# Hybrid streaming encoder, two layers on one core: PSUM tiles from a ring, mixer weights split once and reread as pairs, and a new order of work

## The chip, the core and the metric

The kernel runs on one core of a Trainium2 chip. A core has five engines with queues of their own: TensorE (PE, matmuls; its weight loads are listed as PEld), VectorE (DVE), ScalarE (ACT), GpSimdE (POOL) and SyncE (SP), which here issues every DMA. Matmul results land in PSUM, eight banks of 128 x 512 float32; everything else lives in SBUF or in DRAM. The metric is the time of one execution in device microseconds. The time before is 2417.01 us, the median of three runs (2414.57 to 2417.25).

## What is computed

Two layers run over nine tiles of 128 rows: tiles 0 to 7 are a prompt of 1024 rows, tile 8 holds 8 running streams of 16 rows ("sample"). Model width 1024, feed-forward width 2816 (22 tiles of 128). Cut to what matters here:

```python
def trunk_layer(x, ...):
    xn = rms_norm(x, norm_mix)
    q, k, v, u = split(xn @ w_in)            # 512 | 128 | 128 | 512 columns
    q, k = rope(rms_norm(q)), rope(rms_norm(k))
    attn = sink_attention(q, keys, vals)     # prompt: 64-row chunks, window of 3 chunks
    pool = pool_mixer(u) @ w_pool * scale    # sliding means of 2, 4, 8, 16 rows
    x = x + concat(attn, pool) @ w_out
    h = rms_norm(x, norm_ffn) @ w_up         # 1024 -> 5632
    c = conv3(h)                             # three taps along the rows
    x = x + (silu(gate(c)) * val(c)) @ w_down
```

The sample's tile attends to a cache of 128 rows per stream as well as to its own 16. Rolling caches and states are outputs too.

## The kernel before, in words

All large products are made from float32 operands cut into two parts, hi (rounded to the format that PE reads fast) and lo (the rest): three matmuls, hi*hi, hi*lo and lo*hi (`mm3`, lines 172 to 175). A weight piece of 128 x 512 is loaded into one of five `raw` buffers, cast by ACT (L198) and subtracted by DVE (L199) into a tile of two halves, hi and lo. That is `w_split`.

Each layer has three stages.

- **Mixer.** The nine tiles go in three batches b of three. For each batch there are streams of units: `n` (norm and transposes, L266 to L293), `k` (q, k and v columns: 12 units, three accumulators), `u` (pooling columns: 8 units, two accumulators), `p` (pool matmuls, 4 units, L461), `o` (output projection: 16 units, three accumulators; its first four units and the same in the second half need only the pool part, the others the attention of the batch's three tiles), then `m` (norm for the feed-forward). Attention runs tile by tile as one chain of steps, `L`: preparation a1 to b3, scores, softmax, transposes and values. The sample's tile 8 comes last in that chain. Its step `qk` issues 24 small DMAs (rows of k and v to the outputs and to a tile at partition 0, L699 to L703). Every batch loads and splits the same weight pieces anew: 12 of `w_in` for k, 8 for u and 16 of `w_out`, 36 per batch and 108 per layer.
- **Up.** The up-projection is written as seven products per tile of columns (`PRODUCTS`) on sums and differences of quarters of the input and of the weight, for two halves s of the rows. The sums of the input (`sums(s)`, L325 to L334) are 7 splits and 4 additions of 128 x 1152 per half. `up_post` adds the products up out of PSUM (L943), convolution and gate follow (L990 to L1002), and the result goes to DRAM (`gd`).
- **Down.** In three chunks of the inner dimension, the w_down pieces are split once (`down_prep`, L1044 to L1046) and stay in SBUF. For each of the nine tiles `down_load` fetches the activations from `gd` (L1053), casts and subtracts them (L1055, L1056) and fetches the running x (L1058). The last chunk of layer 0 runs into the mixer of layer 1 (tokens `d`).

What sets the order. A planner (`arrange`) sorts the mixer's steps ("tokens") by keys in a table `PLAN` and takes them in that order as far as their predecessors are done and limits on buffers are kept: among them `mm`, at most four accumulators open at a time. In this list a step's place is its priority; the framework then orders each engine's queue by a schedule of its own in which a step goes as soon as its inputs and buffers are there, the earlier step of the list first. SP's queue, too, is in order: a DMA that waits holds all behind it. `w_advance` asks for weight splits ahead of their unit: two units ahead, four (`LA = 4`) in the middle of the list, where three pieces of seven go into one of the 33 big `B` buffers (`wide`) and the others into five `W` buffers; raw loads go five pieces ahead. Before, the eight PSUM banks are one tile, and the program picks the bank itself: 0 to 3 taken and given back by accumulators (`mm_take`, `mm_give`), 4 and 5 in turn for scores, values and down (`s`), 6 and 7 in turn for transposes and the pool matmuls (`tr`). Up uses banks 0 to 5 as three pairs, one half of the rows in each bank of a pair, and one instruction reads both halves (128 x 576).

Of the kernel before, what the change touches and what calls it, by code (L numbers as in the profile page):

```python
# [17 lines left out]
LA = 4  # L18
# [11 lines left out]
class Weight:  # L30
    def __init__(self, load, n=512, split=True):
        self.load, self.n, self.split, self.wide, self.ahead, self.dve = load, n, split, False, 2, False
# [12 lines left out]
def arrange(tokens, limits):  # L45
# [4 lines left out]
    while left:  # L50
# [7 lines left out]
        for r, n in t.res.items():  # L58
# [7 lines left out]
    dict(k0=(-37.12, 1.06), u0=(-19.58, 1.84), k1=(29.16, 2.63), u1=(73.67, 4.61), o0=(87.72, 2.71),  # L66
         k2=(154.86, 0.47), u2=(167.69, 3.03), o1=(176.8, 5.19), o2=(244.18, 3.8), p0=(39.27, 6.38),
         p1=(90.02, 4.48), p2=(191.64, 17.42), n1=(-29.42, 1.49), n2=(23.54, 3.88), n3=(91.98, 1.07),
         m0=(213.68, 1.15), m1=(240.36, 0.87), m2=(284.99, 1.11), d=(-23.94, 1),
         L=(26.9, 49.72, 64.52, 77.21, 108.8, 144.26, 156.17, 180.28, 202.35, 239.71), cw=(247.35, 4.51),  # L70
         sc=(270.55, 7.25), e_q=1, e_k=0, e_v=0, e_u=0, e_k2=0, e_qt=0, e_pt0=0, e_pt1=0, e_ps0=1, e_ps1=1,
         e_ks=1, e_w=0, e_x0=1, e_x1=0, e_x2=0),
# [11 lines left out]
def encoder_kernel(ctx: ExitStack, tc: tile.TileContext, consts, x_prompt, x_sample, cache_k, cache_v,  # L84
# [15 lines left out]
    BUFS = dict(B=33, W=5, raw=5, PT=4, Q=4, u=2, sA=1, sB=1, D=2, V=5, st=15, ks=1)  # L100
# [17 lines left out]
    psum = ps.tile([128, 8, 512], F32, name="psum")  # L118
    turn = {"s": [4, 5], "tr": [6, 7]}
    mmfree = [0, 1, 2, 3]  # L120

    def P(tag):

        b = turn[tag].pop(0)
        turn[tag].append(b)
        return psum[:, b]

    def mm_take():
        return mmfree.pop(0)
# [21 lines left out]

    state = {}
# [33 lines left out]
    def w_dma(w):  # L186
        w.raw = raw_tile(w.n)
        w.load(w.raw)

    def w_split(w):  # L190
        if not w.split:
            return
        g = T("B" if w.wide else "W", [128, 2, 512], F32R)
        w.hi, w.lo = g[:, 0, 0:w.n], g[:, 1, 0:w.n]
        if w.dve:
            dve.tensor_copy(out=w.hi, in_=w.raw)
        else:
            act.copy(out=w.hi, in_=w.raw)  # L198
        dve.tensor_tensor(out=w.lo, in0=w.raw, in1=f32(w.hi), op=ALU.subtract)  # L199
        w.raw = None  # L200

    def w_advance(pos):
        upto, more = pos + 1, 0
        while upto < len(order) and more < min(order[pos].ahead, order[upto].ahead):
# [139 lines left out]
    def kvq_units(l, b):  # L344
        us = []
        for c, (cols, kn, n) in enumerate(((0, 1, 512), (512, 2, 256))):
            hold = {}
            for j in range(8 // kn):
                def f(w, c=c, kn=kn, n=n, j=j, hold=hold):
                    xT = state["xT", b]  # L350
                    wh, wl = [v.rearrange("p (k n) -> p k n", k=kn) for v in (w.hi, w.lo)]
                    for tl in range(3):
                        t = b * 3 + tl
                        if j == 0:
                            hold[tl] = mm_take()
                        o = psum[:, hold[tl], 0:n]
# [4 lines left out]
                        if (j + 1) * kn == 8:  # L361
# [7 lines left out]
                            mm_give(hold[tl])  # L369
# [3 lines left out]
    def u_units(l, b):  # L373
        us = []
        for c in range(2):
            hold = {}
            for j in range(4):
                def f(w, c=c, j=j, hold=hold):
                    xT = state["xT", b]
                    wh, wl = [v.rearrange("p (k n) -> p k n", k=2) for v in (w.hi, w.lo)]  # L380
                    for s in range(2):
                        if j == 0:
                            hold[s] = mm_take()
                        for kk in range(2):
# [3 lines left out]
                            mm3(psum[:, hold[s], 0:384], a, x, j == 0 and kk == 0, j == 3 and kk == 1)  # L388
                        if j == 3:
                            u_evac(l, b, 2 * c + s, psum[:, hold[s]])  # L390
                            mm_give(hold[s])
# [956 lines left out]
```

## Time and profile before

| | |
|---|---|
| Median of three runs | 2417.01 us |
| Profiled execution | 2412.6 us, its span 2410.8 us |
| PE busy | 2280.5 us, 95% |
| PEld busy | 2025.8 us, 84% |
| DVE busy | 1596.4 us, 66% |
| ACT busy | 959.7 us, 40% |
| Mean granted clock of PE | 0.969 |
| DMA | 271.77 MB, 113 GB/s on average, all on SP's queue but 0.4% of the 16 engines' time |

Busy shares are averages over stages with different limits, so the table of stretches (busy time of each engine between two times, with the granted clock and the DMA engines' share) says more than this one. A matmul's listed duration includes its way through the pipeline; how fast matmuls follow each other is read from their count in a full stretch. The layers lie so: mixer 0 to about 455 us, up to 930, down to about 1215; the same again for layer 1, whose mixer begins under the end of layer 0's down and lasts to about 1645, up to 2121, down to the end.

### The profile page before, as it was taken

To read this page: it belongs to the slowest core of one execution; us is meant where nothing else is said; L and a number is where in the kernel's file an instruction comes from. 1 tells how busy PE (TensorE), PEld (TensorE's weight loads), DVE (VectorE), ACT (ScalarE), POOL (GpSimd) and SP (SyncE) were. 2 spreads that over 40 slices of the span, in tenths; PEclk is the share of its full clock that TensorE was granted. 3 is DMA by queue.
4 is the path that set the end of the run, shared out by engine and by line. 5 is a ranking of instruction groups with operands and counts; after the bars stand their busy time and mean duration, and the time that the engine had idled before them with its cause. 6 is when DMAs were issued, how large, how long until landed. Compare 5 with 4: busy or idle time off the path is not lost.

```text
span 2410.8 us, 35976 instructions
## 1 busy us (share of the span) xinstructions
PE 2280.5 (95%) x13610; PEld 2025.8 (84%) x13610; DVE 1596.4 (66%) x2942; ACT 959.7 (40%) x1774; POOL 201.6 (8%) x411
## 2 busy tenths in 40 slices
PE   7989979899999998999998899788999999989999
PEld 7757757899999997888887687578999999978887
DVE  5766665988888887233356776478888888853332
ACT  4555554534334334121236565454333433421110
POOL 0000000111111110000000000001111111100000
PEclk9989988899999999999999999889999999999999
DMA  6233332222222226364442333422222222273643
GB/s 218 62 112 122 99 117 89 84 79 70 79 75 71 77 75 225 131 218 164 143 135 61 99 127 102 133 89 65 65 80 78 69 79 75 79 246 125 222 157 109
DMA packets 244495, 271.77 MB, mean 113 GB/s; under 512 B 17410, under 2 KB 188370, under 8 KB 244290
## 3 DMA queue, kind: packets, MB, share of 16 engines
q1 hardware_dynamic: 244322, 269.48, 34.9%
q8 instruction: 107, 1.75, 0.3%
q14 instruction: 66, 0.54, 0.1%
HBM read 203.69 MB, written 67.42 MB: 112 GB/s over the span
## 4 chain that ended last, share of the span: by engine, by line
PE 82%; DVE 7%; DMA 5%; ACT 3%; issue 2%; SPq 1%; POOL 0%; ACTq 0%; DVEq 0%
PE psum L173 25%; PE psum L174 25%; PE psum L175 25%; PE psum L658 2%; DMA raw<-in_w_out_dram 2%; DVE W L199 1%; PE psum L305 1%; DVE B L326 1%; DMA raw<-in_w_in_dram 1%; PE psum L645 1%; DMA B<-gd 1%; DMA raw<-in_w_down_dram 1%; DVE B L334 1%; PE psum L461 1%; ACT W L198 1%
## 5 line engine op out<-in xcount | busy, mean ns | idle before, releaser
L173 PE MATMUL psum<-B,W 128*128 128x288 f32 (+1 forms) x1896 | 572.2, 302 | 18.3 <-ACT B L325 12.3
L174 PE MATMUL psum<-B,W 128*128 128x288 f32 (+1 forms) x1896 | 569.9, 301 | 8.1 <-DVE B L326 8.1
L175 PE MATMUL psum<-B,W 128*128 128x288 f32 (+1 forms) x1896 | 568.2, 300 | 0.0
L173 PEld LDWEIGHTS psum<-B,W 128*128 128x128 f32 x1896 | 359.4, 190 | 22.6 <-ACT B L325 13.9
L173 PE MATMUL psum<-B,B 128*128 128x512 f32 (+2 forms) x914 | 357.0, 394 | 20.1 <-ACT B L1055 10.3
L174 PEld LDWEIGHTS psum<-B,W 128*128 128x128 f32 x1896 | 358.8, 189 | 11.2 <-DVE B L326 10.2
L175 PEld LDWEIGHTS psum<-B,W 128*128 128x128 f32 x1896 | 358.9, 189 | 0.9 <-DVE W L199 0.5
L174 PE MATMUL psum<-B,B 128*128 128x512 f32 (+2 forms) x914 | 357.2, 391 | 0.0
L175 PE MATMUL psum<-B,B 128*128 128x512 f32 (+2 forms) x914 | 355.9, 391 | 0.0
L992 DVE SCALAR_TENSOR_TENSOR B<-B,cvp,B 128x1168 f32<-128x1168 f32 x176 | 250.5, 1428 | 7.9 <-ACT B L990 7.7
L173 PEld LDWEIGHTS psum<-B,B 128*128 128x128 f32 x914 | 172.9, 190 | 59.8 <-ACT B L198 11.5
L1083 DVE TENSOR_TENSOR B<-psum,B 128x512 f32<-128x512 f32 x108 | 74.5, 690 | 199.0 <-PE psum L175 198.9
L174 PEld LDWEIGHTS psum<-B,B 128*128 128x128 f32 x914 | 173.5, 190 | 37.6 <-DVE B L199 0.5
L175 PEld LDWEIGHTS psum<-B,B 128*128 128x128 f32 x914 | 172.8, 189 | 37.7 <-issue 0.2
L173 PE MATMUL psum<-W,B 128*128 128x512 f32 (+1 forms) x510 | 190.4, 386 | 9.5 <-ACT B L463 5.0
L199 DVE TENSOR_TENSOR W<-raw,W 128x512 fp32r<-128x512 f32 x184 | 125.8, 689 | 103.4 <-ACT W L198 102.7
L174 PE MATMUL psum<-W,B 128*128 128x512 f32 (+1 forms) x510 | 192.9, 379 | 0.9 <-DVE W L199 0.9
L868 ACT CAST W<-Q 128x512 fp32r<-128x512 f32 x132 | 81.8, 621 | 280.3 <-PE psum L175 280.1
L175 PE MATMUL psum<-W,B 128*128 128x512 f32 (+1 forms) x510 | 191.9, 381 | 0.0
L198 ACT CAST W<-raw 128x512 fp32r<-128x512 f32 x184 | 113.2, 620 | 166.9 <-PE psum L175 58.5
L943 DVE TENSOR_TENSOR B<-psum,PT 128x160 f32<-128x160 f32 (+2 forms) x356 | 147.8, 447 | 27.2 <-PE psum L175 27.1
L943 DVE TENSOR_TENSOR PT<-psum,PT 128x576 f32<-128x576 f32 (+1 forms) x138 | 100.4, 730 | 84.6 <-PE psum L175 84.3
(188 smaller groups left out, 3953.2 us busy)
## 6 DMA issues: line engine op xcount, KB each, us to landing
raw<-in_w_up_dram SPq DMA_DIRECT2D x176, 256.0 KB
xd<-B SPq DMA_DIRECT2D x63, 512.0 KB
B<-xd SPq DMA_DIRECT2D x63, 512.0 KB
raw<-in_w_in_dram SPq DMA_DIRECT2D x120, 256.0 KB
gd<-B SPq DMA_DIRECT2D x44, 576.0 KB
raw<-in_w_down_dram SPq DMA_DIRECT2D x88, 256.0 KB
B<-gd SPq DMA_DIRECT2D x36, 512.0 KB
raw<-in_w_out_dram SPq DMA_DIRECT2D x48, 256.0 KB
```

Source lines behind the costliest of these rows:

```text
L173: pe.matmul(out=out, lhsT=a[0], rhs=b[0], start=first, stop=False)
L174: pe.matmul(out=out, lhsT=a[0], rhs=b[1], start=False, stop=False)
L175: pe.matmul(out=out, lhsT=a[1], rhs=b[0], start=False, stop=last)
L198: act.copy(out=w.hi, in_=w.raw)
L199: dve.tensor_tensor(out=w.lo, in0=w.raw, in1=f32(w.hi), op=ALU.subtract)
L305: pe.transpose(out=tr[:, k * 128:(k + 1) * 128], in_=xn[:, c:c + 128], identity=ident)
L326: dve.tensor_tensor(out=lo, in0=src, in1=f32(hi), op=ALU.subtract)
L658: pe.matmul(out=o, lhsT=V, rhs=H.pop(("p", g, kk)), start=kk == kks[0], stop=kk == 1)
L868: act.copy(out=hi, in_=src)
L943: dve.tensor_tensor(out=o, in0=x, in1=y, op=ALU.add)
L992: dve.scalar_tensor_tensor(out=c, in0=h[:, j:j + 1168], scalar=cvp[:, j, ct:ct + 1], in1=c, op0=ALU.mult, op1=ALU.add)
L1083: dve.tensor_tensor(out=X[:, hs], in0=o, in1=X[:, hs], op=ALU.add)
```

## The change

- **Kept pairs.** Every split piece of k, u and o gets a key (layer, stream, index) and a DRAM tile `wsd[key]`. The first batch that needs it loads, casts and subtracts it as before and then stores the pair hi and lo (512 KB). The other two batches load the pair in one DMA straight into a `W` buffer: no raw load (256 KB), no cast, no subtract.
- **Buffers.** `W` has six buffers for five, `B` 32 for 33; `wide` is gone; the splits, and so the pair loads, are asked for three units ahead (`LA = 3`) throughout.
- **PSUM.** Each use of PSUM takes a tile of one bank from a pool with a tag: `mm` (4 banks), `s` (2), `tr` (2). The pool matmuls move from `tr` to `mm`. The planner has no `mm` limit any more. Up takes one tile for each half of the rows (the third product of three from `s`, the others from `mm`) and reads each half with an instruction of its own, so that each 128 x 576 read becomes two of 128 x 288.
- **Order.** In the attention chain tile 8 comes after tile 5, ahead of tiles 6 and 7; tile 6's preparation is spread over its last steps. All keys of `PLAN` are new, and the sums `s0`, `s1` and up's first weights (`upw`) have keys there. By these keys u2 and the start of o1 stand beside the sample's steps and tiles 6 and 7 beside o1; o2 begins before o1 ends; batch 0's o0 runs interleaved with u1; and up's first weights come last in the layer's list.
- **Up to down.** In up's last tile of columns `down_load` of the first tile is called at product 2, and not in the first down unit; `down_prep` of pieces 0 to 7 is spread over products 1 to 4 and not 0 to 3.

```diff
-LA = 4
+LA = 3
...
-    BUFS = dict(B=33, W=5, raw=5, PT=4, Q=4, u=2, sA=1, sB=1, D=2, V=5, st=15, ks=1)
+    BUFS = dict(B=32, W=6, raw=5, PT=4, Q=4, u=2, sA=1, sB=1, D=2, V=5, st=15, ks=1)
...
     def P(tag):
-        b = turn[tag].pop(0)
-        turn[tag].append(b)
-        return psum[:, b]
+        cnt[0] += 1
+        return ps.tile([128, 512], F32, tag=tag, name=f"{tag}{cnt[0]}", bufs={"mm": 4, "s": 2, "tr": 2}[tag])
...
+    wsd = {(l, x, i): dp.tile([128, 2, 512], F32, name=f"wd{l}{x}{i}")
+          for l in range(DEPTH) for x, n in (("k", 12), ("u", 8), ("o", 16)) for i in range(n)}
+    kept = set()
...
     def w_dma(w):
+        if w.key in kept:
+            return
         w.raw = raw_tile(w.n)
         w.load(w.raw)
...
-        g = T("B" if w.wide else "W", [128, 2, 512], F32R)
+        g = T("W", [128, 2, 512], F32R)
         w.hi, w.lo = g[:, 0, 0:w.n], g[:, 1, 0:w.n]
+        if w.key in kept:
+            sync.dma_start(out=f32(g), in_=wsd[w.key])
+            return
...
         dve.tensor_tensor(out=w.lo, in0=w.raw, in1=f32(w.hi), op=ALU.subtract)
         w.raw = None
+        if w.key is not None:
+            sync.dma_start(out=wsd[w.key], in_=f32(g))
+            kept.add(w.key)
...
-            o = P("tr")[:, 0:384]
+            o = P("mm")[:, 0:384]
             pe.matmul(out=o, lhsT=w.raw, rhs=d, start=True, stop=True)
...
+        seq = (0, 1, 2, 3, 4, 5, 8, 6, 7)
...
-            o = psum[:, 2 * pair + s, 0:QT]
+            o = state["upp", s] = P("s" if (7 * i + n) % 3 == 2 else "mm")[:, 0:QT]
...
+        for s in ss:
+            u = state.pop(("upp", s))
+            x = sum_("sum", s)
+            if n == 0:
+                act.copy(out=x, in_=u)
+            elif n == 1:
+                add(hb_first(row(0), s), [u], [x])
...
                     if i == FT - 1:
-                        for x in (2 * n, 2 * n + 1):
-                            if x < CHUNKS[0][1]:
+                        if n == 2:
+                            down_load(l, 0, 0)
+                        for x in (2 * n - 2, 2 * n - 1):
+                            if 0 <= x < CHUNKS[0][1]:
                                 down_prep(l, x)
...
-        ev = arrange(toks, {"T6": 18, "qkv": 4, "V": BUFS["V"], "mm": 4})
+        ev = arrange(toks, {"T6": 18, "qkv": 4, "V": BUFS["V"]})
```

More of the change, by code (lines that the diff above doesn't have):

```diff
@@ L31, in __init__ @@
     def __init__(self, load, n=512, split=True):
-        self.load, self.n, self.split, self.wide, self.ahead, self.dve = load, n, split, False, 2, False
+        self.load, self.n, self.split, self.dve, self.key = load, n, split, False, None
 class Unit:
@@ L65 @@
 PLAN = [
[L66 to L72, printed above, removed]
@@ L200, in w_split @@
         w.raw = None
+        if w.key is not None:
+            sync.dma_start(out=wsd[w.key], in_=f32(g))
+            kept.add(w.key)
     def w_advance(pos):
         upto, more = pos + 1, 0
-        while upto < len(order) and more < min(order[pos].ahead, order[upto].ahead):
+        while upto < len(order) and more < LA:
             if order[upto].layer != order[pos].layer:
@@ L354, in f @@
                         if j == 0:
-                            hold[tl] = mm_take()
-                        o = psum[:, hold[tl], 0:n]
+                            hold[tl] = P("mm")
+                        o = hold[tl][:, 0:n]
                         for kk in range(kn):
@@ L382, in f @@
                         if j == 0:
-                            hold[s] = mm_take()
+                            hold[s] = P("mm")
                         for kk in range(2):
@@ L387, in f @@
                             x = [xT[i][k // 3][:, k % 3, :] for i in range(2)]
-                            mm3(psum[:, hold[s], 0:384], a, x, j == 0 and kk == 0, j == 3 and kk == 1)
+                            mm3(hold[s][:, 0:384], a, x, j == 0 and kk == 0, j == 3 and kk == 1)
                         if j == 3:
-                            u_evac(l, b, 2 * c + s, psum[:, hold[s]])
-                            mm_give(hold[s])
+                            u_evac(l, b, 2 * c + s, hold[s])
                     if j == 3:
@@ L482, in f @@
                         if j == 0:
-                            hold[tl] = mm_take()
-                        o = psum[:, hold[tl]]
+                            hold[tl] = P("mm")
+                        o = hold[tl]
                         if k >= 4:
@@ L771, in pv @@
             state.pop(("qkv", 8))
-            state.pop(("V", 7))
             state.pop(("V", 8))
@@ L819, in L_steps @@
                 for i, f in enumerate(flat(rest[k])):
-                    put(t, f, (), **(mo if k == 3 and i == 0 else {}))
+                    put(p, f, (), **(mo if k == 3 and i == 0 else {}))
                 more(2 + k)
-            put(t, rest[4], (), **({"V": -1} if t else {}))
-        put(8, sloadv)
-        for f in srest[:-1]:
-            put(8, f)
-        put(8, srest[-1], (), qkv=-1, V=-2, T6=1)
-        kc1 = len(out) - len(srest) + 1
+            put(p, rest[4], (), **({"V": -2 if t == 7 else -1} if t else {}))
         return out, kc1
@@ L926, in up_post @@
     def up_post(l, i, n, ss):
-        pair = (7 * i + n) % 3
-        u = psum[:, 2 * pair:2 * pair + 2]
         last = 1 in ss
@@ L1197, in stream, with keyed @@
                 add(f"{st}.{i}", k + i * step, u, q, (res or {}).get(i))
+        def keyed(x, units, l=l):
+            for i, u in enumerate(units):
+                u.ws[0].key = l, x, i
+            return units
         if l == 0:
@@ L1254, in encoder_kernel @@
                 pre = ([f"s{s}.{i - 1}"] if i else []) + ([ready[i]] if i in ready else [])
-                add(f"s{s}.{i}", (246 if s == 0 else 290) + 3 * i, f, pre)
+                add(f"s{s}.{i}", pl[f"s{s}"][0] + pl[f"s{s}"][1] * i, f, pre)
         for i in range(3):
-            add(f"upw{i}", 286 + 6 * i, lambda l=l, i=i: up_advance(l, i), ["o2.10"])
-        ev = arrange(toks, {"T6": 18, "qkv": 4, "V": BUFS["V"], "mm": 4})
-        lim = [t.name for t in ev].index("spl")
-        wide = [w for t in ev[:lim] for w in t.unit.ws if w.split][12:]
-        for i, w in enumerate(wide[:-6]):
-            w.wide = i % 7 in (2, 4, 6)
-            w.ahead = LA
+            add(f"upw{i}", pl["upw"][0] + pl["upw"][1] * i, lambda l=l, i=i: up_advance(l, i), ["o2.10"])
+        ev = arrange(toks, {"T6": 18, "qkv": 4, "V": BUFS["V"]})
         for t in ev:
```

146 lines of the change are left out of this document (62 added, 84 removed).

## The prediction

> **What bounds the kernel now.** I read the page's busy times first, then the table of stretches by stage, then shorter stretches where TensorE (PE) idles, then the chain and the waits there. In the rows of stretches the columns are: length, busy us (and instructions) of PE, PEld, DVE, ACT, POOL, the granted clock, the DMA engines' share, GB/s.
>
> ```profile
> span 2410.8 us, 35976 instructions
> 10.00:460.00 450.00, 396.00 (x2076) 321.76 (x2077) 302.67 (x765) 236.01 (x568) 34.55 (x32) 0.92 0.36 112
> 460.00:925.00 465.00, 465.00 (x3505) 464.83 (x3504) 399.36 (x582) 188.48 (x249) 65.96 (x166) 1.00 0.25 79
> 925.00:945.00 20.00, 13.61 (x67) 11.53 (x66) 16.30 (x24) 9.37 (x12) 0.77 (x4) 0.83 0.89 286
> 945.00:1215.00 270.00, 270.00 (x1203) 219.89 (x1202) 94.74 (x131) 57.45 (x87) 1.65 (x3) 1.00 0.53 173
> 1215.00:1650.00 435.00, 386.17 (x2027) 312.08 (x2026) 282.48 (x726) 226.58 (x543) 30.96 (x30) 0.93 0.32 98
> 1050.00:1100.00 50.00, 50.00 (x218) 40.49 (x217) 15.40 (x17) 8.33 (x10) 0.00 (x0) 1.00 0.63 201
> 2115.00:2140.00 25.00, 18.83 (x91) 15.98 (x90) 17.87 (x24) 11.18 (x13) 0.77 (x4) 0.86 0.92 296
> ```
>
> The up-projection (460 to 925) and down-projection (945 to 1215) keep PE busy all the time at full clock: nothing is to be had there unless work leaves PE, and none does. The time to win is in the two mixers and the two turns from up to down. I count a stretch's loss as idle PE plus busy PE times the missing clock. First mixer: 54.0 + 0.08 x 396 = 86 us; second: 48.8 + 0.07 x 386 = 76; the turns: 6.4 + 0.17 x 13.6 = 8.7 and 6.2 + 0.14 x 18.8 = 8.8. Together some 180 us of 2411. A 512-wide matmul of the dense down stage takes 50/218 = 0.229 us, so a unit of nine is 2.07 us of PE.
>
> The mixers' loss by place:
>
> ```profile
> 10.00:60.00 50.00, 47.25 (x266) 42.11 (x267) 31.25 (x66) 23.96 (x53) 3.58 (x4) 1.00 0.64 213
> 60.00:160.00 100.00, 82.76 (x418) 65.39 (x417) 73.51 (x248) 59.34 (x165) 9.49 (x6) 0.88 0.27 85
> 320.00:400.00 80.00, 61.69 (x312) 44.00 (x311) 38.01 (x86) 37.38 (x91) 4.45 (x6) 0.84 0.37 114
> 400.00:460.00 60.00, 50.01 (x299) 44.46 (x298) 56.84 (x75) 31.45 (x51) 6.75 (x9) 0.84 0.28 82
> 1260.00:1350.00 90.00, 75.82 (x405) 58.77 (x404) 60.28 (x204) 54.80 (x144) 7.96 (x5) 0.94 0.23 68
> 1510.00:1600.00 90.00, 76.10 (x377) 56.30 (x375) 47.82 (x87) 42.55 (x98) 4.29 (x6) 0.87 0.36 114
> 1600.00:1650.00 50.00, 34.23 (x211) 30.51 (x212) 41.62 (x55) 22.82 (x36) 4.05 (x9) 0.76 0.21 67
> ```
>
> Batch 0 to 1 (60 to 160, 1260 to 1350): 27 + 19 us. Sample attention and the second output projection (320 to 400, 1510 to 1600): 28 + 24. The way into up (400 to 460, 1600 to 1650): 18 + 24. The rest lies scattered. In the last pair DVE is the bound (56.8 of 60 us); in the middle pair no engine is full, so there it is waits:
>
> ```profile
> 99.70 0.63 ACT W L198
> 100.36 0.70 DVE W L199
> 101.08 3.27 DMA raw<-in_w_out_dram
> 104.37 0.63 ACT W L198
> 105.02 0.69 DVE W L199
> ...
> SPq L229 <- DVE W L199: 179.1, 84, 15.4
> SPq L238 <- PE psum L461: 27.6, 5, 15.1
> ```
>
> The first five are from the chain of waits: a raw weight buffer comes free when its split ends, the next load lands 3.27 us later, then cast and subtract: 4.6 us a turn. The last two are the DMA queue's own waits (us in total, times, longest): the in-order SP queue holds weight loads until a raw buffer is free, and a pool weight sitting in that ring holds it until its matmul, once for 15 us.
>
> **The change part by part.** *Splits left out.* Three batches each split 12 k, 8 u and 16 o pieces per layer; batches 1 and 2 now read them as pairs: 72 of 108 per layer, 144 in all.
>
> ```profile
> L199 DVE TENSOR_TENSOR W<-raw,W 128x512 fp32r<-128x512 f32 x184 | 125.8, 689 | 103.4 <-ACT W L198 102.7
> L198 ACT CAST W<-raw 128x512 fp32r<-128x512 f32 x184 | 113.2, 620 | 166.9 <-PE psum L175 58.5 <-DMA raw<-in_w_out_dram 52.2 <-DMA raw<-in_w_in_dram 45.7
> L326 DVE TENSOR_TENSOR B<-B,B 128x1152 fp32r<-128x1152 f32 x14 | 18.7, 1351 | 0.3 <-ACT B L325 0.3
> L334 DVE TENSOR_TENSOR B<-B,B 128x1152 f32<-128x1152 f32 x8 | 10.8, 1353 | 0.1
> ```
>
> That is 144 x 0.689 = 99 us of DVE and 144 x 0.620 = 89 us of ACT, nearly all beside PE work; what counts is that matmuls of batches 1 and 2 no longer stand behind the raw ring or the vector engines and can fill PE while attention waits.
> Middle pair (52 us of loss): PE gets u2, o1 and o2 as free filler, and sample attention no longer comes last, since tiles 6 and 7 follow it. Attention's own chain and the norms stay. I take half: 26.
> Way into up (42 us): the L326 and L334 rows are of 395 to 455 alone and hold both halves' sums, 29.5 us of DVE. The first half's (14.7) can now run under o2, which wants no split; the second half stays behind the last norm. Up's first weight splits now stand last in the layer's list, on the DVE that this frees. Between 0 and 2 x 14.7 I take 20.
> Batch 0 to 1 (46 us): k1's 12 splits leave, 8.3 us of DVE per layer where it is 0.7 busy; o0 is batch 0 and keeps its own. I take 12, and 5 for the scattered rest.
>
> *Down's first load moves ahead.* It now goes out at product 2 of up's last tile, and the weight loads one product later.
>
> ```profile
> 919.09 11.29 SPq L1044 DMA_DIRECT2D raw<-in_w_down_dram  x11
> 930.72 0.38 SPq L1053 DMA_DIRECT2D B<-gd  x1
> ...
> 930.72 5.14 DMA B<-gd
> 935.88 1.05 ACT B L1055
> 936.97 0.79 PE psum L173
> 937.77 0.43 PE psum L174
> ```
>
> Today it queues on SP behind eleven weight loads, lands 5.14 us later, is cast, and PE restarts on a half clock (0.43 a matmul). Product 2 ends some 13 us before up does (24 matmuls a product at 465/3505 = 0.133 us, four products behind it), against 6.2 us for load and cast: covered, if three B buffers are free (there is one fewer). The shifted weights are used one after the other and cost about 1. Of 17.5 I take 15.
>
> *Added traffic.* 72 stores of 512 KB and 144 reads of 512 instead of 256 KB: 37.7 MB more per layer, half written, half read.
>
> ```profile
> raw<-in_w_in_dram SPq DMA_DIRECT2D x120, 256.0 KB
> 330.00:340.00 10.00, 7.88 (x37) 4.90 (x36) 4.22 (x7) 6.31 (x12) 0.56 (x1) 1.00 0.95 321
> 335.67 6.79 SPq L703 DMA_DIRECT2D B<-V  x8
> ```
>
> The fullest 10 us moved 321 GB/s at a share of 0.95, so about 338 is all there is. The first mixer moves 112 x 450 = 50 MB; with 38 more that is 88 MB, 260 us of full DMA in 450: enough on the whole. It is short at the start: 10 to 60 moves 213 x 50 = 10.7 MB, and the 20 stores of k0 and u0 add 10.5: 63 us of transfer in 50. Between 0 (stores slip into the gap behind) and 13 I take 8, since every raw load of this stretch queues among them. By the Trainium skill's DMA: Bandwidth & Descriptors, section "Measured (HBM→SBUF, 128 partitions, SWDGE, issued from GpSimd)", a lone core reaches 425 GB/s with large transfers; by that the start would fit in 50 us and this term would be 0. The row above, the fullest in this trace, decides for 338.
> A store waits on SP for its subtract, and raw loads, X loads and pair reads are queued behind it. The next raw loads wait for the same subtract already (the 179 us above), and five loads are out ahead of it, so I take 0; without that cover it is the third rival. The sample's 24 small transfers (eight took SP 6.79 us) now stand ahead of pair reads of u2 and o1; six W buffers at 2.07 us a unit cover 12 us of them.
>
> *PSUM.* Up reads each product as two 288-wide pieces:
>
> ```profile
> L943 DVE TENSOR_TENSOR PT<-psum,PT 128x576 f32<-128x576 f32 x126 | 95.4, 757 | 84.6 <-PE psum L175 84.3
> L943 DVE TENSOR_TENSOR B<-psum,PT 128x576 f32<-128x576 f32 x84 | 63.2, 752 | 14.0 <-PE psum L175 14.0
> L943 DVE TENSOR_TENSOR B<-psum,PT 128x288 f32<-128x288 f32 x96 | 43.3, 453 | 12.8 <-PE psum L175 12.7
> ```
>
> 210 x (2 x 0.453 - 0.755) = 32 us of DVE, 16 per up stage, whose DVE is busy 399 of 465: hidden under PE; were that cover gone it would cost up to 32. In the mixer the bank limit has left the planner's list: u1 (two accumulators) now runs interleaved with o0 (three) on four banks, and pool matmuls draw from the same ring. Bounds: 0, as other PE work fills, and 4 x 2.07 = 8 a layer, if o0 waits for u1's four last units. I take 2 a layer, near the lower end, because PE keeps the rest of both streams: 4. The transposes' two banks lose the pool matmuls; no row shows a wait for those banks, so I count no gain.
>
> **Sum:** 15 + 26 + 20 + 12 + 5 - 8 - 4 = 66 us less. The profiled execution took 2412.6 us (its span 2410.8 and 1.8 around it), 4.4 under the median of the runs shown, 2417.0. So 2346.6 in its terms, and 2351 as a median.
>
> **The rivals.** *More of the loss goes:* with the mixers' matmuls free of DVE and ACT, 65% of their 162 us leaves: 105 + 15 - 12 = 108, 2309. For it: DVE falls to about 250 of 450 us in the first mixer. Against: attention's chain and the norms are untouched.
> *DMA takes over:* a pair is 524 KB / 338 = 1.55 us of all engines; with the share of 0.35 used by the rest, 1.55 / 0.65 = 2.4 us against the unit's 2.07 when u2, o1 and o2 run back to back: 0.3 x 40 x 2 = 24 us, and the start costs its full 13, 5 more. Gain 66 - 29 = 37: 2380. It decides where pair units follow each other with no attention between.
> *Slower, the store blocks SP:* where DVE's queue puts a split behind softmax by more than the five raw buffers cover (10 us), load, cast and subtract go in series: 4.6 instead of 2.07 us a unit, 2.5 lost. With 27 of batch 0's 72 units so held the gain is gone; with 40, 100 us are lost: 2417 - 66 + 100 = 2451. For it: the longest such wait today is 15.4 us; against: 84 waits share 179, 2 us each.
> *Slower, the bank ring cools PE:* up changes bank at every product, and if PE paused a little at each release and ran at the first mixer's clock of 0.92, two up stages would take 930 x (1/0.92 - 1) = 81 us more: 2432. Against: today's up already cycles through three pairs of banks at 1.00. The Trainium skill's TensorE: Matmul & The Clock Gate, section "A second HAM failure mode: psum-queue depth-cycling", describes such a loss; this trace does not bear it out so far.
> *Little happens:* the stalls are attention's own chain, only the turns gain, 15 - 12 = 3: 2414.
>
> **How the numbers follow.** Forecast 0.60, more 0.12, DMA 0.14, store blocks 0.07, ring cools 0.02, little 0.05. What can be told from no change is about 0.2%, 5 us. Faster 0.60 + 0.12 + 0.14 = 0.86; slower 0.09; same 0.05. The forecast's own range, from its terms' bounds, is 2315 to 2390. The whole range runs from 2305, a little past the "more" case, to 2400, past the DMA case; the last three cases (0.14) stay out.
>
> **What would show it.** Right: in the stretches at each turn PE stays near full and its clock at 1.00; the split's cast and subtract (now L198 and L199) count 72 each; in the two mixers DVE falls by some 50 us each and PE's idle and missing clock by a third to a half; up keeps 3505 matmuls in 465 us. Wrong: PE waiting on a pair's landing (DMA takes over), SP waiting on L199 for far more than 179 us while ACT waits on raw loads (store blocks), a clock below 1.00 in up (ring cools), or the old waits on softmax and norms at the old length (little happens).

## The result and the profile after

The changed kernel takes 2339.1 us (median of four runs, 2338.0 to 2342.5) against 2415.8 for the kernel before on the same chip: a ratio of 0.9685, 95% interval 0.9669 to 0.9702, 77 us less. The forecast was 2351. The profiled execution took 2338.3 us. Its page and its stretches, with the columns of those shown of before (length, PE, PEld, DVE, ACT, POOL, clock, DMA share, GB/s):

```profile
span 2336.4 us, 35965 instructions
PE 2251.6 (96%) x13610; PEld 2009.8 (86%) x13610; DVE 1514.4 (65%) x3015; ACT 877.5 (38%) x1665; POOL 184.4 (8%) x411
```
```profile
10.00:460.00 450.00, 404.34 (x2248) 335.16 (x2249) 277.52 (x728) 211.12 (x513) 35.97 (x40) 0.95 0.57 200
925.00:945.00 20.00, 20.00 (x87) 16.17 (x87) 8.35 (x9) 4.41 (x5) 0.00 (x0) 1.00 0.86 283
1215.00:1650.00 435.00, 413.78 (x2390) 351.54 (x2389) 287.40 (x738) 205.56 (x494) 35.22 (x52) 0.96 0.50 170
2115.00:2140.00 25.00, 25.00 (x110) 20.28 (x109) 6.48 (x11) 4.57 (x8) 0.00 (x0) 1.00 0.39 131
10.00:60.00 50.00, 43.67 (x224) 35.63 (x225) 24.03 (x48) 20.90 (x41) 1.65 (x3) 1.00 0.92 339
60.00:160.00 100.00, 98.50 (x554) 82.56 (x553) 71.83 (x246) 55.09 (x151) 9.87 (x7) 1.00 0.69 249
320.00:400.00 80.00, 69.97 (x363) 56.09 (x362) 46.30 (x86) 38.07 (x80) 4.57 (x6) 0.91 0.50 168
400.00:460.00 60.00, 43.99 (x316) 43.08 (x315) 50.91 (x76) 28.68 (x43) 7.57 (x17) 0.86 0.14 42
1260.00:1350.00 90.00, 86.95 (x463) 71.38 (x462) 57.28 (x182) 43.83 (x115) 5.00 (x3) 1.00 0.71 243
1600.00:1650.00 50.00, 50.00 (x379) 49.98 (x378) 44.06 (x80) 19.22 (x28) 5.28 (x19) 1.00 0.28 90
```

With loss counted as in the prediction, the first mixer's row has 45.7 + 0.05 x 404 = 66 us of it for 86, the second's 21.2 + 0.04 x 414 = 38 for 76 (that row now holds some 70 us of dense up work, because layer 1 runs ahead). Three things stand out. Batch 0 to 1 is nearly full at full clock: 1.5 and 3.1 us are lost for 27 and 19. The start is emptier: 224 matmuls for 266. And layer 0's way into up got no better: 22 us lost (16.0 + 0.14 x 44) for 18.

The stages now come earlier, so a row at the old times holds other work. VectorE's first read of an up result comes 26 us earlier in layer 0 (423.7 us for 450.1) and 70 us earlier in layer 1 (1571.9 for 1641.6). Here are the middle pair and the way into up of after, moved by that much, first layer 0, then layer 1:

```profile
294.00:374.00 80.00, 70.19 (x370) 53.60 (x371) 42.27 (x124) 35.54 (x102) 4.83 (x6) 0.96 0.55 185
374.00:434.00 60.00, 39.03 (x224) 35.16 (x223) 48.28 (x56) 31.49 (x48) 5.86 (x8) 0.80 0.15 52
1440.00:1530.00 90.00, 88.96 (x432) 67.68 (x432) 49.88 (x136) 43.57 (x113) 5.71 (x7) 0.91 0.58 202
1530.00:1580.00 50.00, 37.23 (x235) 33.01 (x234) 41.23 (x50) 25.41 (x40) 4.76 (x7) 0.86 0.24 80
```

By these rows the middle pair loses 13 and 9 us for 28 and 24 before, and the way into up 29 and 18 for 18 and 24.

Four marks, where VectorE reads the last result of up and the first of down, in us from the start. They are starts of timeline rows that join up to three reads, so up's very last read begins 0.2 to 0.6 us later:

| kernel | up 0 ends | down 0 starts | up 1 ends | down 1 starts | span |
|---|---|---|---|---|---|
| before | 929.9 | 945.4 | 2121.3 | 2136.3 | 2410.8 |
| after | 910.3 | 914.9 | 2057.6 | 2062.2 | 2336.4 |

So layer 0's mixer and up gave 20 us; from layer 0's first down result to the end of layer 1's up the time fell from 1175.9 to 1142.7 us, 33 more; the two turns gave 21.

Next what PE waited for most in the way into up, layer 0. The first row is PE's timeline (start, us, engine, line, operation; in brackets the idle time before it and its releaser), the others VectorE's just before:

```profile
424.20 0.61 PE L152 MATMUL mm<-B,W 128*128 128x288 f32 x1 [14.83 <-DVE B L921]
```
```profile
415.96 1.35 DVE L313 TENSOR_TENSOR B<-B,B 128x1152 fp32r<-128x1152 f32 x1
417.23 2.74 DVE L321 TENSOR_TENSOR B<-B,B 128x1152 f32<-128x1152 f32 x2
419.89 3.89 DVE L313 TENSOR_TENSOR B<-B,B 128x1152 fp32r<-128x1152 f32 x3
423.70 0.45 DVE L921 TENSOR_TENSOR B<-mm,PT 128x288 f32<-128x288 f32 x1
```

PE had finished the first half's seven products and the last norm's transposes, and stood for 14.8 us until VectorE read one of those products (line 921), which came only after the second half's sums (lines 313 and 321). In layer 1 the same wait lasted 3.7 us. The longest wait of PE for up's reads was 1.8 us before. The first half's sums, too, came late in layer 0: VectorE took the first of them right behind the last addition of the output projection o2 (line 478).

```profile
384.34 0.68 DVE L478 TENSOR_TENSOR B<-mm,B 128x512 f32<-128x512 f32 x1
384.94 0.14 DVE L254 TENSOR_SCALAR st<-st 128x1 f32<-128x1 f32 x1
385.13 1.36 DVE L313 TENSOR_TENSOR B<-B,B 128x1152 fp32r<-128x1152 f32 x1
```

The waits that the rivals were about (engine, line, waited for: us in total, times, longest), and the two groups of the split:

```profile
SPq L177 <- PE mm L154: 189.0, 100, 18.9
SPq L186 <- DVE W L183: 49.1, 20, 6.9
PE mm L152 <- DMA W<-wd0o: 2.3, 1, 2.3
PE mm L152 <- DMA W<-wd1u: 1.5, 2, 1.3
PE mm L152 <- DMA W<-wd1o: 0.9, 2, 0.8
```
```profile
L183 DVE TENSOR_TENSOR W<-raw,W 128x512 fp32r<-128x512 f32 x72 | 49.2, 687 | 48.1 <-ACT W L182 43.4 <-DMA W<-wd0u 4.4
L182 ACT CAST W<-raw 128x512 fp32r<-128x512 f32 x72 | 44.2, 619 | 67.2 <-PE mm L154 32.8 <-DMA raw<-in_w_in_dram 27.1 <-issue 4.5
```

The first row is pair reads that stand on the SP queue until a matmul gives a `W` buffer back. PE waited under 5 us for pairs, and the SP queue 49 us for a pair to store: neither the DMA engines nor the store took over.

### The profile page after: what moved, and what is told of

Read it like the earlier page. It is cut to its first block, busy times and chain, and to the rows that moved or that the text cites. A ratio compares the mean times of both kernels' runs of the same rounds, so it can differ in the third digit from the quotient of the medians.

```text
span 2336.4 us, 35965 instructions
## 1 busy us (share of the span) xinstructions
PE 2251.6 (96%) x13610; PEld 2009.8 (86%) x13610; DVE 1514.4 (65%) x3015; ACT 877.5 (38%) x1665; POOL 184.4 (8%) x411
## 4 chain that ended last, share of the span: by engine, by line
PE 86%; DVE 6%; DMA 5%; ACT 2%; issue 1%; SPq 0%; POOL 0%; DVEq 0%; ACTq 0%
PE mm L152 14%; PE mm L154 14%; PE mm L153 14%; PE s L154 12%; PE s L152 12%; PE s L153 12%; PE s L642 2%; DMA raw<-in_w_in_dram 1%; PE tr L629 1%; DMA B<-gd 1%; DVE B L313 1%; DMA raw<-in_w_down_dram 1%; PE mm L446 1%; PE tr L565 1%; DVE B L321 1%
## 5 line engine op out<-in xcount | busy, mean ns | idle before, releaser
L152 PE MATMUL mm<-B,W 128*128 128x288 f32 (+1 forms) x1376 | 421.5, 306 | 28.7 <-DVE B L921 18.6
L153 PE MATMUL mm<-B,W 128*128 128x288 f32 (+1 forms) x1376 | 418.1, 304 | 2.1 <-DVE B L313 2.1
L154 PE MATMUL mm<-B,W 128*128 128x288 f32 (+1 forms) x1376 | 417.8, 304 | 0.4
L152 PE MATMUL s<-B,B 128*128 128x512 f32 x792 | 312.3, 395 | 2.1 <-ACT B L1034 1.4
L154 PE MATMUL s<-B,B 128*128 128x512 f32 x792 | 312.4, 394 | 1.1 <-DVE B L1035 1.1
L153 PE MATMUL s<-B,B 128*128 128x512 f32 x792 | 311.8, 394 | 0.0
L152 PEld LDWEIGHTS mm<-B,W 128*128 128x128 f32 x1376 | 261.5, 190 | 34.9 <-DVE B L921 19.0
L153 PEld LDWEIGHTS mm<-B,W 128*128 128x128 f32 x1376 | 261.6, 190 | 3.8 <-DVE B L313 2.5
L154 PEld LDWEIGHTS mm<-B,W 128*128 128x128 f32 x1376 | 261.3, 190 | 1.9 <-DVE W L183 1.7
L152 PE MATMUL mm<-W,B 128*128 128x512 f32 (+1 forms) x576 | 220.8, 388 | 7.8 <-ACT B L279 2.5
L153 PE MATMUL mm<-W,B 128*128 128x512 f32 (+1 forms) x576 | 213.8, 372 | 0.2 <-DVE W L183 0.2
L154 PE MATMUL mm<-W,B 128*128 128x512 f32 (+1 forms) x576 | 213.7, 374 | 0.0
L1060 DVE TENSOR_TENSOR B<-s,B 128x512 f32<-128x512 f32 x108 | 74.2, 688 | 184.4 <-PE s L154 175.4
L152 PEld LDWEIGHTS s<-B,B 128*128 128x128 f32 x792 | 148.7, 188 | 37.2 <-ACT B L1034 1.8
L154 PEld LDWEIGHTS s<-B,B 128*128 128x128 f32 x792 | 148.7, 188 | 36.8 <-DVE B L1035 1.9
L153 PEld LDWEIGHTS s<-B,B 128*128 128x128 f32 x792 | 148.7, 188 | 34.5
L152 PE MATMUL s<-B,W 128*128 128x288 f32 x576 | 171.5, 298 | 2.4 <-ACT B L312 2.4
L153 PE MATMUL s<-B,W 128*128 128x288 f32 x576 | 171.2, 297 | 0.8 <-DVE B L313 0.8
L154 PE MATMUL s<-B,W 128*128 128x288 f32 x576 | 170.9, 297 | 0.0
L1034 ACT CAST B<-B 128x1024 fp32r<-128x1024 f32 (+1 forms) x54 | 52.8, 978 | 242.4 <-DMA B<-gd 160.9
```

The lines of the kernel that those rows point to most:

```text
L152: pe.matmul(out=out, lhsT=a[0], rhs=b[0], start=first, stop=False)
L153: pe.matmul(out=out, lhsT=a[0], rhs=b[1], start=False, stop=False)
L154: pe.matmul(out=out, lhsT=a[1], rhs=b[0], start=False, stop=last)
L1034: act.copy(out=hi, in_=f32(lo))
L1060: dve.tensor_tensor(out=X[:, hs], in0=o, in1=X[:, hs], op=ALU.add)
```

## The experiments

My theory was the prediction's: the pairs free VectorE and ScalarE in the mixers, and most of the mixers' gain hangs on that. The rival: the order does it. All ratios are to the kernel before on the same chip. The profiled executions scatter: two kernels here with the same layer 0 differ there by 6.6 us, so verdicts rest on the ratios, and the traces show where.

| kernel | median us | ratio | 95% interval |
|---|---|---|---|
| `bpairs`: before + pairs | 2404.2 | 0.9965 | 0.9952 to 0.9978 |
| `bdown`: before + turn | 2397.0 | 0.9938 | 0.9922 to 0.9954 |
| `oldorder`: after, order of before | 2386.6 | 0.9890 | 0.9867 to 0.9912 |
| `mmcap`: after, limit back | 2351.1 | 0.9743 | 0.9718 to 0.9768 |
| `t8last`: after, tile 8 last | 2351.2 | 0.9736 | 0.9711 to 0.9761 |
| `nopairs`: after, no pairs | 2345.2 | 0.9714 | 0.9699 to 0.9728 |
| `okeep0`: after, layer 0 keeps o alone | 2339.4 | 0.9686 | 0.9672 to 0.9701 |
| after | 2339.1 | 0.9685 | 0.9669 to 0.9702 |
| `ab33`: after, 33 B buffers | 2334.2 | 0.9673 | 0.9659 to 0.9687 |
| `postfirst`: ab33, first half ahead | 2331.4 | 0.9658 | 0.9632 to 0.9683 |
| `cap1`: after, limit in layer 1 | 2332.0 | 0.9657 | 0.9643 to 0.9672 |
| `noadds`: after, additions left out | 2329.4 | 0.9643 | 0.9627 to 0.9659 |
| `best`: postfirst and cap1 | 2325.6 | 0.9644 | 0.9626 to 0.9663 |

**No pairs in the changed kernel (`nopairs`).**

```diff
-        if w.key is not None:
-            sync.dma_start(out=wsd[w.key], in_=f32(g))
-            kept.add(w.key)
```

> The changed kernel with no pair kept: all 108 pieces of a layer's mixer are loaded raw, cast and subtracted, and nothing is stored; the new order, the PSUM pool, six W buffers and the early down load stay. Theory: the pairs free DVE and ACT in the mixers (72 fewer splits a layer, 82 us of DVE and of ACT in all), and the new order needs that; without them the mixers give back 35 us or more of their 53.6, so 2374 us or over. Rival, the order alone brings it: at most 15 us are given back, 2339 to 2354. Rival, the stores hurt the start: below 2339.

Measured: 0.0029 of ratio given back, 7 us, the two intervals just overlapping. My theory fell: it wanted 35; the rival's bound of 15 holds. The first two stretches of this kernel:

```profile
10.00:60.00 50.00, 47.28 (x260) 41.99 (x261) 32.21 (x71) 25.75 (x54) 4.09 (x4) 1.00 0.63 210
60.00:160.00 100.00, 94.69 (x525) 78.50 (x524) 80.72 (x257) 65.07 (x172) 9.80 (x6) 0.99 0.34 106
```

Its VectorE is busy 1603.9 us in all (1514.4 after), its ScalarE 956.4 (877.5). Without a pair, 60 to 160 is still nearly full (94.7 us at 0.99, for 82.8 at 0.88 before), with VectorE busy 0.81 of the time: PE is filled there without pairs, and the splits go on beside it. That it is the order which fills it does not follow from this row alone (see `oldorder`). The pairs give 554 - 525 = 29 matmuls in that stretch, and their stores cost 260 - 224 = 36 in the one ahead of it.

**The pairs alone on the kernel before (`bpairs`).**

```diff
...
+        if w.key in kept:
+            sync.dma_start(out=f32(g), in_=wsd[w.key])
+            return
...
+        if w.key is not None:
+            sync.dma_start(out=wsd[w.key], in_=f32(g))
+            kept.add(w.key)
```

> The kernel before with only the kept pairs: its order, its PSUM banks, five W buffers with the wide pieces in B, its turn into down. Theory that the pairs bring most of the mixers' gain: 35 to 55 us under before, 2361 to 2381 us. Rival, the order is needed to use the freed time: less than 20 us, 2396 to 2416.

Measured: 8.5 us. With and without the new order the pairs are worth the same 7 or 8, of 77.

**The turn alone on the kernel before (`bdown`).**

```diff
-                        for x in (2 * n, 2 * n + 1):
-                            if x < CHUNKS[0][1]:
+                        if n == 2:
+                            down_load(l, 0, 0)
+                        for x in (2 * n - 2, 2 * n - 1):
+                            if 0 <= x < CHUNKS[0][1]:
...
-                if x == 0:
-                    down_load(l, c, t)
```

> The kernel before with only the turn from up to down changed: the first tile's load at product 2 of the last tile of columns, down's pieces 0 to 7 prepared one product later. The two traces put 20.8 us of the gain at the two turns. Theory that this edit alone makes it: 18 to 21 us under before, about 2396 us. Rival, the forecast's 15 us, the rest being the other PSUM tiles of up: 2401. Rival, the pool's PSUM tiles make it: within 5 us of before.

Measured: 15.0 us (interval 11 to 19), as forecast; of the theory's 18 to 21 only the lower end lies in the interval. The first turn in its trace:

```profile
925.00:945.00 20.00, 18.35 (x93) 15.20 (x92) 18.01 (x29) 10.76 (x15) 1.16 (x4) 1.00 0.89 281
```

18.4 us of 20 at full clock, for 13.6 at 0.83 before. That the marks of after show 21 at the turns is partly how they are taken: they are VectorE's reads, and PE's own loss at the turns was only 17.5 us before.

**The order of before in the changed kernel (`oldorder`)**: keys, chain and planner limit of before.

```diff
...
-        seq = (0, 1, 2, 3, 4, 5, 8, 6, 7)
+        seq = (0, 1, 2, 3, 4, 5, 6, 7, 8)
...
-        ev = arrange(toks, {"T6": 18, "qkv": 4, "V": BUFS["V"]})
+        ev = arrange(toks, {"T6": 18, "qkv": 4, "V": BUFS["V"], "mm": 4})
```

> The changed kernel in the order of before: its keys, its chain with tile 8 last, its planner limit of four accumulators; kept pairs, PSUM pool, six W buffers and the turn into down stay new. The first runs gave the turn 15 us and the pairs alone some 8 of the 75. Theory now, that the new order brings most of the rest: 2380 to 2395 us. Rival, that the PSUM pool or the sixth W buffer brings it, in any order: 2339 to 2355.

Measured: 0.9890, 27 us under before and 50 over the changed kernel. The turn and the pairs by themselves make 23.5 of these 27, so in the old order the PSUM pool, the sixth `W` buffer and the shorter look-ahead make, in sum, no more than what can't be told from nothing. The order makes 50 of the 77 us. It is a bundle: keys, chain and limit, and with the entries of `PLAN` also the choice between VectorE and ScalarE for some copies out of PSUM (`e_q` to `e_x2`), which this run turns back as well and which was not tried apart.

Where the order gains in layer 0 is not where I looked for it. Three rows of `oldorder`, then 160 to 320 of before and of after:

```profile
60.00:160.00 100.00, 93.62 (x508) 75.94 (x506) 64.81 (x230) 52.74 (x148) 8.45 (x6) 0.98 0.60 210
160.00:320.00 160.00, 144.40 (x730) 117.22 (x730) 85.33 (x286) 71.40 (x196) 10.76 (x9) 0.94 0.60 205
320.00:400.00 80.00, 69.14 (x342) 51.88 (x341) 33.92 (x66) 25.86 (x67) 3.45 (x5) 0.83 0.47 161
```
```profile
160.00:320.00 160.00, 154.30 (x789) 125.81 (x788) 103.06 (x295) 83.88 (x213) 10.28 (x7) 0.98 0.35 107
160.00:320.00 160.00, 148.22 (x798) 117.81 (x797) 84.45 (x277) 68.37 (x201) 12.31 (x8) 0.97 0.60 201
```

With the old order, batch 0 to 1 (60 to 160) loses only 8 us of the 27 too. But 160 to 320 then loses 24 for 9 before, and layer 0's up ends at 929.6 us, where it ended before. The new order loses 7, 8 and 6 us less than `oldorder` in the three rows, 21 together; by the marks its up ends 19 us earlier.

**The planner's limit back (`mmcap`)**, all else as after.

```diff
-            kres = {7: {"qkv": 3}, 11: {"V": 3}}
+            kres = {0: {"mm": 3}, 7: {"qkv": 3, "mm": -3}, 8: {"mm": 3}, 11: {"V": 3, "mm": -3}}
...
-            stream(f"o{b}", ou, pre, {15: {"T6": -6}})
+            stream(f"o{b}", ou, pre, {0: {"mm": 3}, 7: {"mm": -3}, 8: {"mm": 3}, 15: {"T6": -6, "mm": -3}})
...
-        ev = arrange(toks, {"T6": 18, "qkv": 4, "V": BUFS["V"]})
+        ev = arrange(toks, {"T6": 18, "qkv": 4, "V": BUFS["V"], "mm": 4})
```

> The changed kernel with one thing back: the planner's limit of four accumulators, so that an output projection and a u stream that want five at once are not mixed. Batch 0 to 1, where PE lost 27 and 19 us before and some 2 and 2 after, mixes o0 and u1. Theory, that the mixing is what fills PE there: 20 to 40 us over the changed kernel, 2359 to 2379. Rival, that the keys alone do it: within 6 us, 2333 to 2345.

Measured: 14 us over the changed kernel, less than I had put on it and more than the rival allows. Layer 0 of this kernel:

```profile
60.00:160.00 100.00, 93.70 (x520) 78.15 (x519) 71.48 (x251) 54.95 (x153) 9.95 (x6) 0.97 0.59 208
320.00:400.00 80.00, 63.84 (x316) 46.92 (x315) 34.58 (x87) 29.18 (x74) 3.75 (x5) 0.89 0.54 183
```

That is 34 and 47 matmuls fewer than after (in the first row 9 us lost for 1.5); its layer 0 up ends at 929.8 us, where it ended before, not at 910.3. But from there to the end of layer 1's up it takes 1134.1 us (934.4 to 2068.5), 8.6 less than after. The limit hurts in one layer and helps in the other.

**The sample's tile last again (`t8last`).**

```diff
-        seq = (0, 1, 2, 3, 4, 5, 8, 6, 7)
+        seq = (0, 1, 2, 3, 4, 5, 6, 7, 8)
```

> The changed kernel with the sample's tile last in the attention chain again; all keys as they are. Theory, that the sample ahead of tiles 6 and 7 gives the middle pair's gain (some 30 us by the two traces): 2355 to 2370 us. Rival, that tiles 6 and 7 leave the same holes where they come last, or that the keys do it: within 6 us of 2339.

Measured: 12 us over the changed kernel, between the two. Here 1350 to 1550 of this kernel, then of after:

```profile
1350.00:1550.00 200.00, 186.00 (x978) 146.76 (x977) 103.14 (x299) 86.82 (x237) 12.18 (x12) 0.94 0.54 183
```
```profile
1350.00:1550.00 200.00, 192.90 (x1039) 153.87 (x1038) 110.67 (x311) 90.79 (x247) 14.91 (x15) 0.94 0.56 192
```

With the tile last, 25 us are lost there for 19.

**A 33rd B buffer (`ab33`)**, against the 14.8 us wait.

```diff
-    BUFS = dict(B=32, W=6, raw=5, PT=4, Q=4, u=2, sA=1, sB=1, D=2, V=5, st=15, ks=1)
+    BUFS = dict(B=33, W=6, raw=5, PT=4, Q=4, u=2, sA=1, sB=1, D=2, V=5, st=10, ks=1)
```

> The changed kernel with 33 B buffers for 32 (and 10 small statistics tiles for 15, to make room). In its layer 0 PE stands 14.8 us for the first product that goes into a B row, and DVE is at the second half's sums all that time. Theory: the row waits for a B buffer that only the end of those sums gives back; with one more the row is there early, the stall goes, and the time falls by 8 to 15 us, to 2324 to 2331. Rival: DVE takes its work in list order, and the row's sum stands behind the second half's sums whatever buffers there are; the time stays within 3 us of 2339.

Measured: 0.9673, not told apart from after. The wait view of its way into up:

```profile
PE mm L152 <- DVE B L921: 14.8, 1, 14.8
```

The wait is the same to the tenth: a missing buffer was not its cause.

**The first half's products ahead of the second half's sums (`postfirst`)**, on `ab33`. `tail` is the second half's sums from the third on, `ups` is up's list of units.

```diff
...
-        events += [t.unit for t in ev]
...
+        events += [t.unit for t in ev[:cut] if t.name[:3] != "upw"]
+        events += [t.unit for t in ev[cut:] if t.name[:3] not in ("s1.", "upw")]
+        events += up_ev + ups[:7] + tail
...
-        events += up_units(l)
+        events += ups[7:]
```

> The changed kernel with 33 B buffers and 10 st tiles, as in the run before, and up's first seven units (first half of the rows) put into the list ahead of the second half's sums from the third on; two F tiles are given back earlier to make room. The run with 33 buffers left the 14.8 us wait on the first B row as it was, so its cause is DVE's order: the reads of the first half's products stand behind 16 us of the second half's sums. Theory: put ahead of them, the wait goes and PE starts the second half as each sum comes: 12 to 20 us for both layers, 2315 to 2325. Rival: the sums of the second half then come later by as much as the reads take, and PE waits for them: within 4 us of 2335.

Measured: 0.9658, 3.6 us under `ab33`, with intervals that overlap by most of their length. In its wait view of the same stretch the wait on the product's read is gone, and these stand in its place:

```profile
PE s L152 <- ACT B L312: 4.2, 2, 2.4
PE mm L152 <- ACT B L312: 4.0, 5, 1.4
PE mm L153 <- DVE B L313: 4.0, 3, 1.9
```

The cause of the wait was right, VectorE's order, and the gain was not: PE now waits for the sums themselves (lines 312 and 313), as the rival had it.

**The second half's additions left out (`noadds`).** The code has four of them in each layer (line 321); the expectation counts five.

```diff
-                dve.tensor_tensor(out=F(*o), in0=F(*a), in1=F(*b), op=op)
+                if s == 0:
+                    dve.tensor_tensor(out=F(*o), in0=F(*a), in1=F(*b), op=op)
```

> The changed kernel without the five additions of the second half's sums (line 321), in both layers: 5 x 1.37 us of DVE work is left out, and the half's operands are not the right ones. In the way into up layer 0's DVE is busy 50.9 of 60 us while PE idles 16. Theory, that DVE's amount of work is the bound there: about 6.9 us in each layer, 2323 to 2328. Rival, that the order and waits between ACT, DVE and PE set it: within 4 us of 2339.

Measured: 10 us, of 10.8 left out (eight times 1.35). The wait, on the same line of code, in its trace:

```profile
PE mm L152 <- DVE B L922: 9.4, 1, 9.4
```

It is 5.4 us shorter, four additions of 1.36. So the wait follows VectorE's amount of work, and the total fell by nearly all of what was left out. The place does not fit: by the marks the gain lies in layer 1 (1133.1 us from down 0 to the end of up 1, for 1142.7), and layer 0's up ended 4.5 us later, in one profiled execution and within the scatter of 6.6. That VectorE's amount of work is the bound in layer 0 is therefore likely and not shown.

**Layer 0 keeps only the o pairs (`okeep0`).**

```diff
-        if w.key is not None:
+        if w.key is not None and (w.key[0] == 1 or w.key[1] == "o"):
```

> The changed kernel with layer 0 keeping only the o pairs: its k and u pieces are split anew in every batch and not stored; layer 1 keeps all. Without any pairs, layer 0's PE did 260 matmuls in 10:60 against 224 with them, and 525 against 554 in 60:160, so that both stood alike at 160 us. Theory, that the stores of the start take back there what the pairs give in batch 1: the start is faster by some 5 us and 60:160 slower by as much, the sum within 4 us of 2339. Rival, that the stores of the start are a net loss: 2328 to 2334. Second rival, that the pairs of k and u are a net gain in layer 0: 2343 or over.

Measured: 0.9686 against 0.9685, nothing. Its first stretches:

```profile
10.00:60.00 50.00, 46.51 (x259) 41.51 (x260) 32.38 (x70) 25.53 (x53) 4.09 (x4) 1.00 0.63 211
60.00:160.00 100.00, 94.70 (x527) 78.45 (x526) 80.59 (x257) 65.16 (x171) 9.81 (x6) 1.00 0.48 159
```

The start gains 35 matmuls and batch 1 loses 27: in layer 0 the k and u pairs pay for themselves and no more.

**The limit in layer 1 alone (`cap1`)**: `mmcap`'s edit with

```diff
-        ev = arrange(toks, {"T6": 18, "qkv": 4, "V": BUFS["V"]})
+        ev = arrange(toks, {"T6": 18, "qkv": 4, "V": BUFS["V"], "mm": 4 if l == 1 else 99})
```

> The changed kernel with the planner's limit of four accumulators back in layer 1 alone. With the limit in both layers, the stretch from layer 0's first down result to layer 1's last up result took 1134.1 us against 1142.7, and the stretch before it 934.4 against 914.9. Theory, that the limit costs in layer 0, where batch 0's o0 and u1 stand side by side, and helps in layer 1: 8 us under the changed kernel, 2329 to 2333. Rival, that the difference in layer 1 is the run's chance: within 4 us of 2339.

Measured: 6.8 us under the changed kernel. 1300 to 1400 of this kernel and of after:

```profile
1300.00:1400.00 100.00, 97.05 (x533) 80.01 (x532) 62.33 (x204) 53.13 (x147) 8.28 (x6) 1.00 0.63 218
```
```profile
1300.00:1400.00 100.00, 94.75 (x501) 76.34 (x500) 64.38 (x209) 50.96 (x140) 8.01 (x6) 0.98 0.65 218
```

It does 32 matmuls more here and loses 3 us for 7. With `mmcap`'s 14 us over after, the limit's lift is worth some 21 us in layer 0 and costs 7 in layer 1, if the layers add.

**Both edits together (`best`)**: `postfirst` with `cap1`'s limit.

> The two edits that came out ahead of the changed kernel, together: 33 B buffers with up's first seven units ahead of the second half's sums (2331.4 us against before's 2415.2, ratio 0.9658) and the limit of four accumulators in layer 1 alone (2332.0, ratio 0.9657; the changed kernel 0.9685). If they act at places of their own (the way into up; layer 1's batches), the ratio is about 0.9630, 2325 us. Rival, that both only move the same waits of layer 1's mixer: 0.9657, 2332 us.

Measured: 2325.6 us, 0.9644, by the ratios 10 us under the changed kernel (13 by the medians). It beats both kernels. Whether its parts add is not settled: 0.9644 lies between the two expectations, and its interval holds both.

## Why the prediction came out right, and for which reasons

The time was right: 2351 forecast, 2339 measured, in the range, faster. The mechanism that I put most of it on was not, and that the sum still came out is in good part luck: terms that were too large and too small made up for each other.

- **The turns, 15:** right. The edit alone gave 15.0, and PE stays at 20.00 of 20 and 25.00 of 25 us, clock 1.00.
- **The start, -8:** right in its place, 266 - 224 = 42 matmuls before and after, of them 36 by the stores (36 x 0.229 = 8.2 us). What I left out is that batch 1 gives it back by 160 us. My capacity of 338 GB/s was too low: the row it came from is not the fullest of before's trace, as the last section shows. The Trainium skill's DMA: Bandwidth & Descriptors, section "Measured (HBM→SBUF, 128 partitions, SWDGE, issued from GpSimd)", has 425 GB/s for a transfer of 16 MB; by that, an estimate, the stores would have gone through at no loss. It has 341 for one of 1 MB, and the weight pieces and pairs here are of 512 KB or less; the trace has the loss, at a mean of 339 GB/s, although 10 us of it reach 403.
- **Batch 0 to 1, 12:** the failed step was "k1's 12 splits leave": the stretch gained 26 and 16 us, and layer 0 has 21 of the 26 without any pairs (5.3 idle and 0.01 of the clock are lost there). It has 19 of the 26 with the old order (`oldorder`) and 18 with the limit back (`mmcap`), but only 4 with the pairs alone (`bpairs`: 82.53 us busy at 0.93). What those three share ahead of this row and `bpairs` lacks is the PSUM pool, the sixth `W` buffer and the shorter look-ahead; which of them fills the row was not tried. The order adds the last 7, and under it less is lost again from 160 to 320 us (16 us for 24 in `oldorder`).
- **The bank ring in the mixer, -4:** wrong in sign. I priced the wait of o0 for u1's banks and not what the mixing fills: lifting the limit, which lets u1 and o0 mix, is worth 14 us over both layers.
- **The middle pair, 26:** the size was near, 30 by the moved rows (28 + 24 before, 13 + 9 after), but its two causes stood in one term. The order of the sample is worth 12 of it; the freed splits are within the 7 that all pairs make; the rest was not tried apart.
- **The way into up, 20:** failed, at the step "the first half's (14.7) can now run under o2". In layer 0 of after these sums begin right behind o2's last addition (line 478), and before they had run under o2 already, from 400.0 to 420.2 us with o2's last addition at 421.4; what holds them back was not tried. From that addition to VectorE's first read of up it takes 39.4 us there, for 28.7 before. In layer 1 of after they do run partly under o2 (from 1526.4 us, o2's last addition at 1544.2), and it takes 27.7 for 39.8. So one layer lost what the other gained; by the moved rows the loss of both went from 42 to 47 us. In layer 0 PE then also runs out of products that VectorE has read, behind the second half's 16 us of sums. I had looked at what leaves VectorE, not at what is late next.
- **VectorE:** 288-wide reads cost 28 us more over both up stages (line 921 against line 943 of before), forecast 32, and up stayed full at clock 1.00. In all, VectorE's busy time fell by 82 us, 41 a layer, where my sign of being right was some 50 in each mixer. The split groups count 72 each, at lines 182 and 183; the prediction had their new line numbers wrong.
- **The rivals:** the DMA's takeover and the blocked store are refuted by the waits above. The ring that cools PE is refuted too: in up, from 470 to 900 us and from 1620 to 2040, each stretch of 10 us holds 77 or 78 matmuls at clock 1.00. The Trainium skill's TensorE: Matmul & The Clock Gate, section "A second HAM failure mode: psum-queue depth-cycling", describes such a loss, for matmuls of bf16; this trace does not show it. "More goes" is half true: 36% of the mixers' loss went ((162 - 104)/162, by rows that hold more of up than before's), not 65%.

How the 77 us divide by the runs: turn 15, order 50 (the limit 14 and tile 8 another 12 of it; the remaining 24 the keys and the choice of engine for the copies, if these add up, which was not tried), pairs 7 to 8, and about 4 unassigned. That the keys need the PSUM pool, since five accumulators can't be held under the old bank list, was not tried apart; nor was the new order under before's PSUM list and buffers, so the 50 us may hang on these as well.

## What to carry to other kernels

In this kernel, where no engine was full and PE idled, taking work off the helper engines gained little by itself (7 us for 90 us of VectorE and 79 of ScalarE); a list that offers PE other ready work gained much (50 us). So price "what else could PE do here" ahead of "what leaves the other engines". Switch each part off alone before crediting it, and follow a gain past its own stretch: a forecast can have the sum right with its terms swapped, and what is gained in one stretch can be lost in the next. And where a step is moved earlier, look at the in-order engine behind it for the next thing that is late.

## What the runs showed of the hardware

The DMA engines went well over the 338 GB/s that I had drawn from before. Two stretches of after:

```profile
30.00:40.00 10.00, 10.00 (x66) 9.01 (x65) 2.08 (x3) 3.82 (x7) 0.00 (x0) 1.00 0.98 382
50.00:60.00 10.00, 8.56 (x53) 7.72 (x52) 6.76 (x17) 4.57 (x10) 0.55 (x1) 1.00 1.04 403
```

Before's own trace had gone over it: the row of 321 GB/s is not the fullest there, as this one in layer 0's down shows.

```profile
1140.00:1150.00 10.00, 10.00 (x45) 8.11 (x44) 3.62 (x5) 1.67 (x2) 0.00 (x0) 1.00 1.05 368
```

Shares of 0.95 to 1.05 stand beside 321 to 403 GB/s, so a full share does not say how many GB/s there are; the mix of transfers differs, and the runs don't show what in it decides.

A PE that is busy by its records can still lose its clock. Around the sample's value product (64 matmuls of 64 columns) in layer 1 of after:

```profile
1440.00:1450.00 10.00, 10.00 (x61) 7.75 (x61) 1.39 (x3) 2.63 (x5) 0.00 (x0) 0.79 0.94 378
1450.00:1460.00 10.00, 10.00 (x47) 7.24 (x45) 2.84 (x11) 3.19 (x13) 0.00 (x0) 0.50 0.03 9
```

No idle time, and half a clock. The same product in layer 1 of before (its second half), and in layer 0 of after (its first half; the second ran at 1.00 too):

```profile
1556.00:1564.00 8.00, 8.00 (x35) 5.05 (x35) 0.62 (x1) 0.70 (x2) 0.00 (x0) 0.50 0.55 173
```
```profile
282.00:290.00 8.00, 8.00 (x52) 5.91 (x51) 1.40 (x3) 1.17 (x2) 0.00 (x0) 1.00 0.53 155
```

So it happens with some of these stretches and not with others; what decides was not tried. Counting loss as idle PE plus missing clock catches it, counting idle time alone does not.
